# A hybrid RG-LRU and attention block on one core: PSUM reads behind a slot's steps outside the tail, query stores on SyncE, other slots for the odd bank and the gates

## The chip, the core and the metric

The kernel runs on one core of a Trainium2 chip. A core has five engines, each with an instruction queue of its own that it works off in order: TensorE (PE, matrix products into PSUM), VectorE (DVE), ScalarE (ACT), GpSimd (POOL) and SyncE (SP), which here only issues DMAs; ScalarE issues some too. The metric is the time of one execution on the device in microseconds (us), lower is better.

## The reference

One decoder block over 2048 positions of width 1024, in fp32, with these steps (cut):

```
shift, scale, gate = split(silu(c) @ w_mod + b_mod)
h = rms_norm(x) * (1 + scale) + shift
rnn_x, rnn_gate, q, k, v, attn_gate, merge_r, merge_a = split(h @ w_in)      # w_in: 1024 x 8192
y = rg_lru(causal_conv(rnn_x), ...) * silu(rnn_gate)                         # scan along the sequence
o = mixture of three dilated windows of attention(rope(q), rope(k), v) * silu(attn_gate)
m = sigmoid(merge_r) * (y @ w_out_rnn) + sigmoid(merge_a) * (o @ w_out_attn)
out = rms_norm(x + gate * (m @ w_o))
```

## The kernel before

**Products.** The normalized h is held transposed, the sequence in four banks of 512 columns; a half `f` (0 or 1) works on an even and an odd bank. An fp32 product is made of three passes over high and low parts (`mm3`: high x high, high x low, low x high), and ScalarE writes the high part of a weight tile `S`, GpSimd (in the tail of the second half VectorE) the low part: this is a split. Two blocks of rows times two banks are done as one scheme of seven products (`strassen`), in PSUM banks X, Z, W, V, X, Y and V again; the seventh is held back (`behind`) and issued by `last_product` behind the first or second product of the next scheme. One product is twelve matmuls of 128x128 by 128x512, issued by `prod`.

**Order.** There is one order of all instructions, written by hand. `prod` counts products in `n_prod`; a step put into `late[n]` or `after_prod[n]` is issued by `run_late(n)` after product n, and "slot n" of a stage means behind its n-th product (`later(n, fn)`). Each engine receives its instructions in the order in which this code issues them. `prod` also evicts the product (the `evict` that it is given: a copy on ScalarE or a sum on VectorE frees the PSUM bank), loads the next `S` where one is free (`load_free`) and splits the weights that are `ahead` products in front (`split_next`). In the first half the eviction is issued behind the slot's steps, in the second half ahead of them. All DMAs rotate over eight completion semaphores, so one waits in its queue for the one eight before it to land.

**Stages of the second half**, by the span's time: `second_heads` (about 700 to 766 us) runs 20 products, the first and fifth of ten schemes, while `build_odd_late` builds the second half's odd bank: the rows in `x3` are squared and summed on ScalarE (`square`), scaled on VectorE (`scale_rows`, by `rstd_first` and `rstd_last`) and transposed by TensorE from slot 6 on (`ODD_AT`). The gates' stage (`hu`, to 907 us) does the rest of these schemes and sends gates to DRAM through three buffers `ev`; beside it run `residual_gate` (the gate's column sums: loads `gw`, sums `ga`, a row `gateD`) and `rotary_tables` (angles, sines, and four `piece`s: repeat, transpose by TensorE, store). The recurrent stage (`rp`, to 1266 us) does the RG-LRU: gates from small products, sigmoids on ScalarE, the scan on VectorE (L1154), and value blocks, which TensorE transposes (L1356) and ScalarE evicts (L1360). The tail (`qp`, to 1374 us) does a rotated query block, a value block, a rotated key block and two more; beside it `gated_weight` makes four groups of the output weight times the gate (loads `wo`, products with `gb`, sums `ws`, stores to `oD`), and `rotated_pairs` stores rotated queries and keys (`qT`, `kT`). Attention follows from 1374 us.

Lines used below: L163 high part (ScalarE), L169 low part (GpSimd), L172 low part (VectorE), L410 and L411 copies and sums of a scheme, L501 the last sum of a scheme, L561 to L581 building a bank, L894 scaling rows, L1027 squares, L1229 and L1234 a table piece, L1273 to L1309 rotation and its stores, L1339 unrotated query and key stores, L1445 and L1449 gates and their stores, L1511 to L1540 the gated groups.

Of the kernel before, what the change touches and what calls it, by code (L numbers as in the profile page):

```python
# [21 lines left out]
P = 128  # L22
# [68 lines left out]
def decoder_block(ctx, tc, x, c, positions, g_norm, w_mod, b_mod, w_in, b_gate, conv_w, conv_b,  # L91
# [296 lines left out]
    def prod(op, ps, b, first, last, evict):  # L388
        f, i, s = op
        bh, bl = B[b]  # L390
        for k in range(KH):
            mm3(ps[:], s[:, 0, k, :], s[:, 1, k, :], bh[:, k, :], bl[:, k, :],
                first=first and k == 0, last=last and k == KH - 1, skip_group_check=True)
        n_prod[0] += 1
        if f:
            evict()
            used.add(i)
            load_free()
            split_next(i + 4)
        run_late(n_prod[0])  # L400
        if f:
            load_free()
            split_next(i + 4)
        else:
            evict()

    def kept_sum(u, ps, of=None):

# [15 lines left out]
    def strassen(up, f, key, done, u1=None):  # L424

        x, X = pair_id[key], None
        if u1 is None:
            X = T(pj, [P, CH], F32, "X", bufs=2)
            u1 = T(up, [P, CH], F32, "u1", bufs=1)
            prod(take(f, x, 0), X, "B11", True, False, kept_sum(u1, X) if f else last_product)  # L430
            if f:
                last_product()
            else:
                kept_sum(u1, X)()
        Z = T(pj, [P, CH], F32, "Z")
        u2 = T(up, [P, CH], F32, "u2", bufs=2)
        prod(take(f, x, 1), Z, "T2", True, True, kept_sum(u2, Z, u1))
        last_product()
        W = T(pj, [P, CH], F32, "W")
        u3 = T(up, [P, CH], F32, "u3", bufs=1)  # L440
        prod(take(f, x, 2), W, "T3", True, True, kept_sum(u3, W, u2))
        tag = "V" if X is not None else next(body_tags)
        V = T(pj, [P, CH], F32, tag, bufs=1 + (tag == "X"))
        prod(take(f, x, 3), V, "T1", True, False, lambda: done(1, 1, V, u3))
        if X is not None:
            prod(take(f, x, 4), X, "B21", False, True, lambda: done(0, 0, X, None))
        Y = T(pj, [P, CH], F32, "Y")
        prod(take(f, x, 5), Y, "T4", True, True, lambda: done(1, 0, Y, u3))
        op = take(f, x, 6)
        behind.append(lambda: prod(op, V, "B22", False, True, lambda: done(0, 1, V, u2)))  # L450
# [567 lines left out]
    def second_heads(up, st):  # L1018
# [8 lines left out]
            nc.scalar.activation(jk[:], x3[r], AF.Square, accum_out=ss[:, 0, r : r + 1])  # L1027

        for r in range(4):
            plan[1 + r].append(lambda r=r: square(r))  # L1030
        plan[4].append(lambda: rstd_first(ss))
        plan[5].append(lambda: rstd_last(ss))
        plan[5].append(lambda: scale_rows(x3, ss, range(2)))
        plan[6].append(lambda: scale_rows(x3, ss, range(2, 4)))
        for n in ODD_AT:
            plan[n].append(lambda: next(odd))
        for n, fns in plan.items():
# [139 lines left out]
    def rotary_tables(rp, f):  # L1177
# [69 lines left out]
        base = n_prod[0]  # L1247
        for x, fn in enumerate((angles, None, products, *reduce(TWO_PI * 4096, 7, 8), None, *reduce(TWO_PI, 11, 5), quarter, sines)):
            if fn:
                after_prod.setdefault(base + (9 + x if f else TABLES + 7 * (x // 2) + 2 * (x % 2)), []).append(fn)  # L1250

        for x, (q, i) in enumerate((q, i) for q in range(2) for i in range(2)):
            for d, fn in zip((0, 2, 3), piece(q, i)):
                after_prod.setdefault(base + (34 + 3 * x if f else PIECES[x]) + d, []).append(fn)

    def load_tables(qp, f):
        Ct = T(qp, [P, HALF], F32, "Ct")
# [23 lines left out]
    def rotated_pairs(qp, f, Ct, St):  # L1281

        for base, dstT, qs in QK:
            made = [0]

            def rotated(i, j, ps, u, dstT=dstT, qs=qs, made=made):
# [19 lines left out]
                def store():  # L1306
                    for hh in range(4):
                        r0 = (4 * i + hh) * P
                        (nc.scalar if f else nc.sync).dma_start(dstT[r0 : r0 + 32, :, n * P : (n + 1) * P],  # L1309
                                          v[0][hh * 32 : (hh + 1) * 32, :].rearrange("p (r j) -> p r j", r=4))  # L1310

                steps_after(n_prod[0], ((wait, shuffle), (wait + 1, turn), (wait + 2, add), (wait + 3 + f, store)))
# [147 lines left out]
    def later(d, fn):  # L1460

        late.setdefault(n_prod[0] + d, []).append(fn)

    def residual_gate(ep):
# [2 lines left out]
        w, row = {}, {}  # L1467

        def at_slot(i, fn):
            later(i + 6, fn)  # L1470

        def piece():
            return T(ep, [P, CH], F32, "gw", bufs=3)
# [24 lines left out]
        for q in range(2):  # L1498
            for k in range(KT):
                i = KT * q + k  # L1500
                at_slot(i, lambda q=q, k=k: load(q, k))
                at_slot(i + 2, lambda q=q, k=k: add(q, k))
            at_slot(12 + 9 * q, lambda q=q: total(q))
            at_slot(14 + 9 * q, lambda q=q: bias(q))

    O_PART = {"T1": 0, "T2": 1, "T4": 2, "T3": 3, "B11": (0, 0), "B21": (1, 0), "B22": (1, 1)}

    def gated_weight(ep):
# [5 lines left out]
        def group(k):  # L1514
# [23 lines left out]
            def store_sums():  # L1538
                nc.scalar.dma_start(oD[k, :, :2, :], v["t"][:])
                nc.scalar.dma_start(oD[k, :, 2:, :], v[1][:])  # L1540

            return ((0, load), (3, lambda: gate(0)), (4, lambda: gate(1)), (5, lambda: sums(0)),
                    (6, lambda: sums(1)), (7, store_sums))

        for k, i in enumerate((3, 10, 17, 24)):
            for d, fn in group(k):
                later(i + d, fn)

    def next_norm():

# [21 lines left out]
    def next_even():  # L1572
# [19 lines left out]
            later(4 + i, load)  # L1592
        for i in range(NS):
            late.setdefault(N1 + 1 + i - NS, []).append(load_next)
            if i < NS - 3:
                late.setdefault(N1 + 2 + i - NS, []).append(lambda i=i: split_next(i))


    def touch(pool, tags):
# [8 lines left out]
    for f in range(2):  # L1608
# [39 lines left out]
        plain_pool[0] = qp  # L1648
        plain_at[0] = lambda: T(qp, [P, CH], F32, "t0", bufs=NT0)

        touch(qp, (("u1", 1), ("u2", 2), ("u3", 1), ("t0", NT0), ("t1", NT1[f])))
        tabs = load_tables(qp, f)
        if f:
            low_part_by[0] = lo_dve
            gated_weight(qp)
            after_prod.setdefault(N1 + len(ops2) - 7, []).append(load_first_y)
# [886 lines left out]
```

## Time and profile before

| what | value |
|---|---|
| time, median of 3 runs | 2213.46 us (2209.07 to 2214.8) |
| the profiled execution's own time | 2211.68 us |
| its span | 2209.9 us |
| granted TensorE clock, mean | 0.992 |
| TensorE busy | 2158.4 us (98%) |
| VectorE, ScalarE, GpSimd busy | 1523.4, 1261.9, 1205.7 us |
| DMA moved | 510.70 MB, mean 231 GB/s |

A row of a timeline begins with its start and its length in us, then engine, line of the kernel, operation, what it writes `<-` what it reads, the shape and the count of instructions put together. Square brackets give the idle time of that engine ahead of the row and what ended it. "SPq" and "ACTq" are DMA issues on the queues of SyncE and ScalarE. Buffer numbers are left out in the profile.

### The profile page before, as it was taken

What the parts mean: (1) busy time and instruction counts of PE and PEld (TensorE: products, weight loads), DVE (VectorE), ACT (ScalarE), POOL (GpSimd) and SP (SyncE); (2) the same over time, 40 slices, a digit from 0 to 9 for tenths busy, and PEclk for the clock granted to TensorE, in tenths of its full rate; (3) what the DMA queues carried; (4) which work ended last, traced back from release to release, by engine and by line L of the source; (5) the groups of instructions that cost most, each with busy time, mean ns of one, the idle gap of its engine ahead of it and who ended that gap; (6) DMA issues with size and microseconds to landing.
All of it is one profiled execution on the core that took longest, in us unless ns stands there. A gap on an engine that the chain in (4) does not pass through costs nothing. (4 is left out here: it accounts for less than half of the span.)

```text
span 2209.9 us, 33475 instructions
## 1 busy us (share of the span) xinstructions
PE 2158.4 (98%) x10965; PEld 1816.8 (82%) x10965; DVE 1523.4 (69%) x2513; ACT 1261.9 (57%) x2547; POOL 1205.7 (55%) x884
## 2 busy tenths in 40 slices
PE   8999999999999999999999999999999999999998
PEld 6998888888887787888888777888889898978787
DVE  6769788978576854345656668466677778746887
ACT  4547667667534523376766622567677877632443
POOL 2477777677566322355555511356565657433886
PEclk9999999999999999999999999999999999999999
DMA  8355665665986599979784478989888888789653
GB/s 294 110 167 196 212 200 192 204 227 191 269 261 184 147 331 317 289 235 269 241 257 131 129 235 247 290 266 289 275 273 265 246 257 257 229 285 282 190 172 134
DMA packets 455574, 510.70 MB, mean 231 GB/s; under 512 B 91784, under 2 KB 334692, under 8 KB 454632
## 3 DMA queue, kind: packets, MB, share of 16 engines
q1 hardware_dynamic: 423748, 426.30, 64.1%
q10 hardware_dynamic: 31460, 82.22, 9.8%
q8 instruction: 87, 1.43, 0.3%
q14 instruction: 87, 0.71, 0.1%
q0 software_dynamic: 192, 0.05, 0.0%
HBM read 334.38 MB, written 174.07 MB: 230 GB/s over the span
## 5 line engine op out<-in xcount | busy, mean ns | idle before, releaser
L169 POOL TENSOR_TENSOR S<-R,S 128x512 fp32r<-128x512 f32 x254 | 375.7, 1484 | 322.7 <-ACT S L163 272.2
L155 PE MATMUL X<-T,S 128*128 128x512 f32 x1440 | 348.2, 391 | 0.0
L155 PE MATMUL V<-T,S 128*128 128x512 f32 x1344 | 326.7, 392 | 2.1 <-ACT T L163 1.2
L155 PEld LDWEIGHTS X<-T,S 128*128 128x128 f32 x1440 | 270.6, 189 | 56.9 <-issue 0.9
L155 PEld LDWEIGHTS V<-T,S 128*128 128x128 f32 x1344 | 252.1, 189 | 55.5 <-ACT T L163 1.6
L155 PE MATMUL pj<-yh,S 128*128 128x512 f32 x848 | 285.9, 396 | 3.9 <-ACT yh L163 2.6
L169 POOL TENSOR_TENSOR S<-s,S 128x512 fp32r<-128x512 f32 x117 | 186.9, 1598 | 99.8 <-ACT S L163 70.3
L163 ACT ACTIVATE S<-R 128x512 fp32r<-128x512 f32 x266 | 163.8, 621 | 92.7 <-DMA R<-in_w_in_dram 36.2
L155 PEld LDWEIGHTS pj<-yh,S 128*128 128x128 f32 x848 | 159.5, 189 | 37.7 <-ACT yh L163 4.8
L155 PE MATMUL Z<-T,S 128*128 128x512 f32 x768 | 187.6, 394 | 0.0
L155 PE MATMUL W<-T,S 128*128 128x512 f32 x768 | 185.0, 390 | 1.1 <-DVE ev L1445 1.1
L1778 ACT ACTIVATE pp<-pp,st 128x256 f32<-128x256 f32 (+3 forms) x256 | 133.4, 523 | 75.3 <-DVE st L1777 74.7
L155 PE MATMUL Y<-T,S 128*128 128x512 f32 x720 | 173.6, 390 | 0.6 <-POOL S L169 0.6
L155 PEld LDWEIGHTS Z<-T,S 128*128 128x128 f32 x768 | 145.4, 190 | 30.3
L155 PEld LDWEIGHTS W<-T,S 128*128 128x128 f32 x768 | 143.9, 188 | 31.4 <-ACT u1h L410 1.5
L155 PE MATMUL pj<-yl,S 128*128 128x512 f32 x424 | 166.0, 394 | 1.2 <-POOL yl L169 0.9
L155 PEld LDWEIGHTS Y<-T,S 128*128 128x128 f32 x720 | 134.8, 188 | 30.2 <-POOL S L169 1.1
L163 ACT ACTIVATE S<-s 128x512 fp32r<-128x512 f32 x126 | 78.7, 625 | 140.4 <-DVE s L304 44.3
L172 DVE TENSOR_TENSOR ptl<-pT,pth 128x384 fp32r<-128x384 f32 (+1 forms) x160 | 97.8, 628 | 49.2 <-ACT pth L163 46.9
L1777 DVE CUSTOM_DVE_ANT_0 pp<-sc,msk 128x256 f32<-128x256 f32 (+3 forms) x256 | 104.2, 449 | 35.8 <-PE sc L155 33.6
L1842 ACT ACTIVATE pp<-pp,M 128x256 f32<-128x256 f32 (+3 forms) x256 | 118.1, 524 | 9.2 <-DVE M L1966 9.2
L169 POOL TENSOR_TENSOR vh<-vraw,vh 128x256 fp32r<-128x256 f32 (+1 forms) x64 | 66.0, 1031 | 99.4 <-ACT vh L163 77.9
(444 smaller groups left out, 4680.4 us busy)
## 6 DMA issues: line engine op xcount, KB each, us to landing
sD<-S ACTq DMA_DIRECT2D x112, 512.0 KB, 3.7
S<-sD SPq DMA_DIRECT2D x112, 512.0 KB, 5.4
S<-wD SPq DMA_DIRECT2D x100, 512.0 KB, 6.4
R<-in_w_in_dram SPq DMA_DIRECT2D x182, 256.0 KB, 4.0
wD<-s ACTq DMA_DIRECT2D x64, 256.0 KB, 5.2
T<-in_w_mod_dram SPq DMA_DIRECT2D x8, 1024.0 KB
zaT<-ev SPq DMA_DIRECT2D x32, 256.0 KB, 2.9
yaT<-zs SPq DMA_DIRECT2D x32, 256.0 KB, 3.4
```

The costliest lines, as they stand in the source:

```text
L155: nc.tensor.matmul(o, lhsT=l, rhs=r, start=st, stop=sp, **kw)
L163: nc.scalar.activation(o, i, AF.Copy)
L169: nc.gpsimd.tensor_tensor(o, i, h.bitcast(F32), ALU.subtract)
L172: nc.vector.tensor_tensor(o, i, h.bitcast(F32), ALU.subtract)
L1777: nc.vector.tensor_tensor_reduce(pdst, s_ps, mask, 1.0, 3e38, ALU.add, ALU.min, m_)
L1778: nc.scalar.activation(pdst, pdst, AF.Exp, bias=m_, scale=-1.0, accum_out=l_)
L1842: nc.scalar.activation(pp, pp, AF.Copy, scale=w)
```

## The change

It adds and removes no arithmetic and moves instructions only:

1. In the second half `prod` evicts behind the slot's steps too, as the first half did; only in the tail (`tail[0]`) it evicts first. `strassen` likewise.
2. In the 20 products of the heads, splits go 2 products ahead instead of 4; `next_even` makes three first splits at the last three slots instead of four, of which the first was three slots sooner.
3. The odd bank: two squares a slot in slots 1 and 2, scalings in slots 4 and 5 instead of 5 and 6.
4. The second half's rotary tables and their pieces come 8 slots sooner.
5. Rotated queries are stored from SyncE's queue in both halves; keys of the second half stay on ScalarE's.
6. `residual_gate` loads in slots 6 to 28 instead of 6 to 21, adds three slots behind its load instead of two, and makes its sums in slots 21 and 34 instead of 18 and 27.
7. `gated_weight` loads its groups in slots 0, 8, 16, 24 instead of 3, 10, 17, 24, with one more slot between the load and the first product.
8. `touch` sets aside the space of `wo` and `ws` ahead of `Ct`, `St` and `gb`.

```diff
             mm3(ps[:], s[:, 0, k, :], s[:, 1, k, :], bh[:, k, :], bl[:, k, :],
                 first=first and k == 0, last=last and k == KH - 1, skip_group_check=True)
         n_prod[0] += 1
+        if tail[0]:
+            evict()
+        ahead = 2 if i < 2 * N_HEADS else 4
         if f:
-            evict()
             used.add(i)
             load_free()
-            split_next(i + 4)
+            split_next(i + ahead)
         run_late(n_prod[0])
         if f:
             load_free()
-            split_next(i + 4)
-        else:
+            split_next(i + ahead)
+        if not tail[0]:
             evict()
+
+    tail = [False]
 
     def kept_sum(u, ps, of=None):
...
         if u1 is None:
             X = T(pj, [P, CH], F32, "X", bufs=2)
             u1 = T(up, [P, CH], F32, "u1", bufs=1)
-            prod(take(f, x, 0), X, "B11", True, False, kept_sum(u1, X) if f else last_product)
-            if f:
+            prod(take(f, x, 0), X, "B11", True, False, kept_sum(u1, X) if tail[0] else last_product)
+            if tail[0]:
                 last_product()
             else:
                 kept_sum(u1, X)()
...
             nc.scalar.activation(jk[:], x3[r], AF.Square, accum_out=ss[:, 0, r : r + 1])
 
         for r in range(4):
-            plan[1 + r].append(lambda r=r: square(r))
-        plan[4].append(lambda: rstd_first(ss))
-        plan[5].append(lambda: rstd_last(ss))
-        plan[5].append(lambda: scale_rows(x3, ss, range(2)))
-        plan[6].append(lambda: scale_rows(x3, ss, range(2, 4)))
+            plan[1 + r // 2].append(lambda r=r: square(r))
+        plan[3].append(lambda: rstd_first(ss))
+        plan[4].append(lambda: rstd_last(ss))
+        plan[4].append(lambda: scale_rows(x3, ss, range(2)))
+        plan[5].append(lambda: scale_rows(x3, ss, range(2, 4)))
         for n in ODD_AT:
             plan[n].append(lambda: next(odd))
         for n, fns in plan.items():
...
         base = n_prod[0]
         for x, fn in enumerate((angles, None, products, *reduce(TWO_PI * 4096, 7, 8), None, *reduce(TWO_PI, 11, 5), quarter, sines)):
             if fn:
-                after_prod.setdefault(base + (9 + x if f else TABLES + 7 * (x // 2) + 2 * (x % 2)), []).append(fn)
+                after_prod.setdefault(base + (1 + x if f else TABLES + 7 * (x // 2) + 2 * (x % 2)), []).append(fn)
 
         for x, (q, i) in enumerate((q, i) for q in range(2) for i in range(2)):
             for d, fn in zip((0, 2, 3), piece(q, i)):
-                after_prod.setdefault(base + (34 + 3 * x if f else PIECES[x]) + d, []).append(fn)
+                after_prod.setdefault(base + (26 + 3 * x if f else PIECES[x]) + d, []).append(fn)
 
     def load_tables(qp, f):
         Ct = T(qp, [P, HALF], F32, "Ct")
...
                 def store():
                     for hh in range(4):
                         r0 = (4 * i + hh) * P
-                        (nc.scalar if f else nc.sync).dma_start(dstT[r0 : r0 + 32, :, n * P : (n + 1) * P],
+                        (nc.scalar if f and dstT is kT else nc.sync).dma_start(dstT[r0 : r0 + 32, :, n * P : (n + 1) * P],
                                           v[0][hh * 32 : (hh + 1) * 32, :].rearrange("p (r j) -> p r j", r=4))
 
                 steps_after(n_prod[0], ((wait, shuffle), (wait + 1, turn), (wait + 2, add), (wait + 3 + f, store)))
...
         w, row = {}, {}
 
         def at_slot(i, fn):
-            later(i + 6, fn)
+            later(6 + 3 * i // 2, fn)
 
         def piece():
             return T(ep, [P, CH], F32, "gw", bufs=3)
...
                 i = KT * q + k
                 at_slot(i, lambda q=q, k=k: load(q, k))
                 at_slot(i + 2, lambda q=q, k=k: add(q, k))
-            at_slot(12 + 9 * q, lambda q=q: total(q))
-            at_slot(14 + 9 * q, lambda q=q: bias(q))
+            at_slot(10 + 9 * q, lambda q=q: total(q))
+            at_slot(13 + 9 * q, lambda q=q: bias(q))
 
     O_PART = {"T1": 0, "T2": 1, "T4": 2, "T3": 3, "B11": (0, 0), "B21": (1, 0), "B22": (1, 1)}
...
                 nc.scalar.dma_start(oD[k, :, :2, :], v["t"][:])
                 nc.scalar.dma_start(oD[k, :, 2:, :], v[1][:])
 
-            return ((0, load), (3, lambda: gate(0)), (4, lambda: gate(1)), (5, lambda: sums(0)),
-                    (6, lambda: sums(1)), (7, store_sums))
-
-        for k, i in enumerate((3, 10, 17, 24)):
+            return ((0, load), (4, lambda: gate(0)), (5, lambda: gate(1)), (6, lambda: sums(0)),
+                    (7, lambda: sums(1)), (8, store_sums))
+
+        for k, i in enumerate((0, 8, 16, 24)):
             for d, fn in group(k):
-                later(i + d, fn)
+                later(i + d, fn) if i + d else fn()
 
     def next_norm():
...
             later(4 + i, load)
         for i in range(NS):
             late.setdefault(N1 + 1 + i - NS, []).append(load_next)
-            if i < NS - 3:
-                late.setdefault(N1 + 2 + i - NS, []).append(lambda i=i: split_next(i))
+            if i < 3:
+                late.setdefault(N1 + i - 2, []).append(lambda i=i: split_next(i))
 
 
     def touch(pool, tags):
...
         plain_pool[0] = qp
         plain_at[0] = lambda: T(qp, [P, CH], F32, "t0", bufs=NT0)
 
-        touch(qp, (("u1", 1), ("u2", 2), ("u3", 1), ("t0", NT0), ("t1", NT1[f])))
+        touch(qp, (("u1", 1), ("u2", 2), ("u3", 1), ("t0", NT0), ("t1", NT1[f]),
+                   *((("wo", 2, 2, CH), ("ws", 1, 2, CH)) if f else ())))
         tabs = load_tables(qp, f)
         if f:
+            tail[0] = True
             low_part_by[0] = lo_dve
             gated_weight(qp)
             after_prod.setdefault(N1 + len(ops2) - 7, []).append(load_first_y)
```

The order written out shows what this moves at three places. In the first, VectorE late in the recurrent stage, `y<-a,htail` is the scan, `u<-Z` and `u<-W` are evictions of products of the scheme that runs then. Before:

```order
L317 TENSOR_TENSOR s_2150_11447<-R_2144_11418,s_2150_11447 128x512
L411 TENSOR_TENSOR u_2178_11589<-Z_11588,u_2167_11531 128x512
L1153 TENSOR_TENSOR t_11515<-t_11515,gi_11469 128x512
L1154 SCALAR_TENSOR_TENSOR y_11468<-a_11514,htail_199,t_11515 128x512
L411 TENSOR_TENSOR u_2184_11616<-W_11615,u_2178_11589 128x512
L1159 TENSOR_TENSOR zs_11337<-y_11468,zs_11337 128x512
```

After:

```order
L317 TENSOR_TENSOR s_2150_11446<-R_2144_11417,s_2150_11446 128x512
L505 TENSOR_TENSOR ev_11585<-V_11453,u_2142_11398 128x512
L1157 TENSOR_TENSOR t_11513<-t_11513,gi_11467 128x512
L1158 SCALAR_TENSOR_TENSOR y_11466<-a_11512,htail_199,t_11513 128x512
L415 TENSOR_TENSOR u_2178_11589<-Z_11588,u_2167_11531 128x512
L1163 TENSOR_TENSOR zs_11351<-y_11466,zs_11351 128x512
L415 TENSOR_TENSOR u_2184_11616<-W_11615,u_2178_11589 128x512
```

The scan and the product ahead of it now stand in front of the eviction of Z, and the last eviction of V stands behind L317.

The second place is ScalarE in the tail; `t<-pg` are evictions of transposed values, `qT<-t` stores of rotated queries, `oD` the stores of the first gated group. Before:

```order
L163 ACTIVATE S_2261_11979<-s_2241_11848 128x512
L1539 DMA oD<-ws_11951 128x1024
L1540 DMA oD<-wo_11845 128x1024
L1309 DMA qT<-t_2250_11907 128x1x128 x4
L1309 DMA qT<-t_2254_11930 128x1x128 x4
L1273 ACTIVATE t_2274_12053<-X_11913 128x512
L410 ACTIVATE u_2284_12092<-X_12091 128x512
L1309 DMA qT<-t_2269_12013 128x1x128 x4
L1360 ACTIVATE t_2285_12112<-pg_12083 128x512
L1360 ACTIVATE t_2290_12139<-pg_12115 128x512
L1309 DMA qT<-t_2276_12058 128x1x128 x4
L1360 ACTIVATE t_2294_12168<-pg_12142 128x512
```

After:

```order
L1543 DMA oD<-ws_11911 128x1024
L1544 DMA oD<-wo_11801 128x1024
L163 ACTIVATE S_2263_11968<-R_2204_11719 128x512
L1282 ACTIVATE t_2260_11957<-t_2260_11957 128x512
L163 ACTIVATE S_2266_11988<-s_2244_11851 128x512
L1277 ACTIVATE t_2277_12056<-X_11920 128x512
L414 ACTIVATE u_2287_12096<-X_12095 128x512
L1364 ACTIVATE t_2289_12118<-pg_12087 128x512
L1364 ACTIVATE t_2293_12144<-pg_12121 128x512
```

The sixteen stores of queries are gone from this queue, and the stores to `oD` come two splits sooner.

The third place is SyncE's queue at the same time; the three `S` loads in a row are those of the rotated key's first products. Before:

```order
L1511 DMA gb_11794<-gateD 128x1024
L260 DMA R_2235_11826<-in_w_in_dram 128x4x128
L1521 DMA wo_11843<-in_w_o_dram 128x1024
L1521 DMA wo_11845<-in_w_o_dram 128x1024
L339 DMA S_2262_11982<-sD 128x1024
L339 DMA S_2263_11984<-sD 128x1024
L339 DMA S_2266_12001<-sD 128x1024
L1521 DMA wo_12005<-in_w_o_dram 128x1024
L1521 DMA wo_12007<-in_w_o_dram 128x1024
L339 DMA S_2272_12031<-sD 128x1024
```

After:

```order
L1515 DMA gb_11797<-gateD 128x1024
L1525 DMA wo_11799<-in_w_o_dram 128x1024
L1525 DMA wo_11801<-in_w_o_dram 128x1024
L260 DMA R_2240_11833<-in_w_in_dram 128x4x128
L1525 DMA wo_11961<-in_w_o_dram 128x1024
L1525 DMA wo_11963<-in_w_o_dram 128x1024
L339 DMA S_2267_11991<-sD 128x1024
L339 DMA S_2268_11993<-sD 128x1024
L339 DMA S_2271_12010<-sD 128x1024
L1313 DMA qT<-t_2254_11914 128x1x128 x4
L339 DMA S_2275_12034<-sD 128x1024
L1313 DMA qT<-t_2258_11938 128x1x128 x4
```

The second group's `wo` loads have moved from behind the three `S` loads to ahead of them, the first group's ahead of the raw load `R`, and the query stores stand between later `S` loads.

## Prediction

> **What bounds the kernel now.** The first line of the page gives the span, the row of busy times the engines, and these two show that TensorE is the bound:
>
> ```profile
> span 2209.9 us, 33475 instructions
> PE 2158.4 (98%) x10965; PEld 1816.8 (82%) x10965; DVE 1523.4 (69%) x2513; ACT 1261.9 (57%) x2547; POOL 1205.7 (55%) x884
> ```
>
> TensorE works for 2158.4 of 2209.9 us, so only its 51.5 us of waiting can be won by moving other engines' work. Next I asked what TensorE waited for between 680 us (end of the first half) and 1380 us (attention has begun), where every edit lies:
>
> ```profile
> PE pg L1356 <- ACT t L1360: 4.8, 1, 4.8
> PE pg L1356 <- ACT y L1129: 3.4, 2, 1.9
> PE pg L561 <- DVE T L894: 2.5, 3, 1.3
> PE pj L155 <- ACT yh L163: 2.0, 1, 2.0
> PE pg L1234 <- DVE ev L1229: 1.8, 1, 1.8
> PE pg L1356 <- ACT sg L1360: 1.7, 1, 1.7
> PE pg L561 <- DVE t L581: 1.5, 2, 0.7
> PE V L155 <- ACT T L163: 1.2, 1, 1.2
> PE W L155 <- DVE ev L1445: 1.1, 1, 1.1
> ...
> ```
>
> Columns: who waited, for whom, us in total, times, longest. These nine make 20.0 us. A longer wait costs more than itself, as three stretches of the table by stretches show, right behind waits of 1.9, 4.8 and 1.8 us (the number after POOL's count is the clock granted to TensorE), and the products in them:
>
> ```profile
> 1252.40:1257.30 4.90, 4.84 (x17) 3.92 (x18) 0.00 (x0) 1.18 (x3) 1.29 (x1) 0.65 0.16 59
> 1315.90:1322.00 6.10, 6.07 (x17) 4.96 (x18) 0.00 (x0) 1.06 (x2) 0.00 (x0) 0.52 1.05 279
> 870.00:873.00 3.00, 3.00 (x16) 2.53 (x17) 1.12 (x2) 1.25 (x2) 0.85 (x1) 1.00 1.04 409
> 1252.87 4.58 PE L155 MATMUL V<-T,S 128*128 128x512 f32 x12
> 1263.11 3.02 PE L155 MATMUL V<-T,S 128*128 128x512 f32 x12
> 1316.70 5.33 PE L155 MATMUL Z<-T,S 128*128 128x512 f32 x12
> ```
>
> Twelve matmuls behind transposes take 3.02 us at full clock (1263.11), but 4.58 and 5.33 where the clock was 0.65 and 0.52: 1.6 and 2.3 us more. The Trainium skill ("TensorE: Matmul & The Clock Gate", HAM oscillation) gives as rule that TensorE should have no idle gaps above about 3.4 us. By that rule the wait of 1.9 would not slow what follows, its 1.6 us would not come back, and the sum below would be -17.1 in place of -18.7; the row has the clock at 0.65 behind 1.9 us and at 1.00 behind 1.8, so here the rows decide.
>
> **The change part by part.** No arithmetic is added or removed; every term is a wait. Durations are those of the profiled execution, 2211.68 us (2209.9 and 1.8 around it), which is 1.8 below the median of the runs shown.
>
> *Later splits at the turn of the halves.* The two waits for DVE t (1.5 us) stand behind ScalarE's splits, which wait for raw loads in front of the next bank's build, as in the second of two places:
>
> ```profile
> 693.82 0.63 ACT L163 ACTIVATE S<-R 128x512 fp32r<-128x512 f32 x1 [4.18 <-DMA R<-in_w_in_dram]
> ```
>
> The change puts three splits at the last slots in place of four up to three slots sooner, so the builds no longer stand behind a load that is on its way: -1.5.
>
> *Odd bank scaled sooner.* In slot 6 the transposes wait for the scaling, and the scaling had been waiting for the squares:
>
> ```profile
> 712.90 1.05 ACT L1027 ACTIVATE t<-T 128x1024 bf16<-128x1024 f32 x1
> 715.72 4.78 DVE L894 TENSOR_SCALAR T<-T,ss 128x1024 f32<-128x1024 f32 x4
> 717.13 0.27 PE L561 MATMUL pg<-cs,T 128*128 128x128 f32 x1
> 725.50 0.60 PE L561 MATMUL Y<-cs,T 128*128 128x128 f32 x4
> 729.15 0.60 PE L561 MATMUL pg<-cs,T 128*128 128x128 f32 x4
> ```
>
> Slot 6 takes 725.50 - 717.13 = 8.37 us, slot 7, which has as many transposes, 3.65: a loss of 4.7. Two squares to a slot end the last square some 6 us sooner (four of some 1.2 us with the reading of the sum, between 702 and 708, two evictions among them), and VectorE, idle there, ends its four scalings of 1.2 at about 714, where slot 6 now begins at 715.6. The whole 4.7 comes back: -4.7.
>
> *Steps before evictions, outside the tail.* The recurrence's scan stands behind the eviction of Z on VectorE, ScalarE waits for the scan, then loads a table and evicts the bank that TensorE's transposes need:
>
> ```profile
> 1243.99 0.63 ACT L1149 ACTIVATE t<-t 128x512 f32<-128x512 f32 x1
> 1248.88 1.28 DVE L1154 TENSOR_TENSOR_SCAN y<-a,htail,t 128x512 f32<-128x512 f32 x1
> 1250.20 0.20 ACT L1157 ACTIVATE htail<-y 128x1 f32<-128x1 f32 x1 [3.57 <-DVE y L1154]
> ```
>
> With the scan ahead of Z's eviction, the square root (done at 1244.6) and VectorE's work before it set it: it ends near 1248.1 instead of 1250.2, and the transposes wait 0.1 in place of 1.9. The other wait of this kind (3.4 - 1.9 = 1.5) goes likewise; of that for sg (1.7), which stands behind VectorE's eviction of V, I take half. Here: 1.5 + 1.8 + 1.6 (clock) + 0.9 = -5.8. What is late next are the evictions; nothing reads the Z bank for five products. That the order as such is harmless can be read in the first half, which has had it always; in 70 to 680 us TensorE's longest wait was this:
>
> ```profile
> PE V L155 <- DVE xr L501: 0.5, 1, 0.5
> ```
>
> *Rotated queries stored by SP.* ScalarE issues 16 stores of queries, and its evictions stand behind them until buffers have landed:
>
> ```profile
> 1299.84 7.00 ACTq L1309 DMA_DIRECT2D qT<-t  x8
> 1306.95 0.60 ACT L1273 ACTIVATE t<-X 128x512 f32<-128x512 f32 x1 [9.19 <-DMA qT<-t]
> 1315.28 0.60 ACT L1360 ACTIVATE t<-pg 128x512 f32<-128x512 f32 x1 [6.70 <-DMA qT<-t]
> ```
>
> TensorE's transposes need the bank that ScalarE frees with the eviction at 1315.28. Off that queue ScalarE can do it at about 1308.5, when it waits only for a t0 buffer that VectorE frees: -4.85 - 2.3 = -7.2. The 16 issues (eight took 7.00 us on ScalarE) now lie on SP's queue, behind the loads of S for the rotated key's first three products and ahead of later ones.
>
> *Gated groups.* Group 1's two loads now stand on SP ahead of three loads of S, and the second of them waits until group 0's store has landed:
>
> ```profile
> 1298.76 0.68 DVE L1536 TENSOR_TENSOR wo<-wo,ws 128x512 f32<-128x512 f32 x1
> 1288.41 8.48 SPq L339 DMA_DIRECT2D S<-sD  x3
> DMA to landing us min/median/max: 3.0/6.4/8.4
> DMA to landing us min/median/max: 6.6/6.6/6.6
> 1290.93 2.88 PE L155 MATMUL Z<-T,S 128*128 128x512 f32 x12
> 1304.89 3.00 PE L155 MATMUL X<-T,S 128*128 128x512 f32 x12
> ```
>
> Group 0's last sum (1298.76) comes nine instructions of about 0.7 sooner, near 1292.5; its store is landed 3.0 to 6.4 us later by the first row on landing (1295.5 to 1299), the loads of S are issued some 0.5 us after and land 6.6 later by the second: 1302.6 to 1306, against need at 1304.9. An added wait, then: between 0 and 1.2 + 2.3 (clock) = 3.5; the middle is just in time, I take +0.5. VectorE's first gating now stands ahead of two low parts of S and waits for wo: issued near 1276 and landed 6.6 later, as S is, so that the parts are done by 1288, and the product that reads the first of them begins at 1290.93. At the end of the tail the wait for yh (2.0) is for this store buffer; the space now lies elsewhere, but the last store is a slot later: between 0 and -2.0, I take -1.0.
>
> *Split-ahead of 2 instead of 4 in the heads.* VectorE has hardly a gap there, and splits of S wait on ScalarE behind its work:
>
> ```profile
> 730.60:766.00 35.40, 33.06 (x149) 26.83 (x148) 34.75 (x42) 21.82 (x39) 12.34 (x9) 1.00 0.51 146
> ```
>
> Between 0 and +4.7 (the two waits of 1.1 and 1.2 there, twice more), I take +1.0; most products find their split a product early.
>
> *Gate sums and tables.* Same loads, spread over 22 slots for 15; tables move eight slots forward, where three ev buffers are shared with gates whose stores land late. At the old place:
>
> ```profile
> 868.86 0.96 DVE L1229 COPY ev<-co 128x512 f32<-128x512 f32 x1 [2.85 <-ACT ev L1440]
> ```
>
> Between -1.8 (the wait for ev goes) and +5.4 (all four table pieces wait 1.8): I take 0, between the two, since the buffers are as scarce at the new place, by the row at the slower rival.
>
> Sum: -1.5 - 4.7 - 5.8 - 7.2 + 0.5 - 1.0 + 1.0 + 0 = -18.7 us. 2211.68 - 18.7 = 2193.0; against the median 2213.46 - 18.7 = 2194.8. I say 2194.
>
> **Rivals.** *The heads give back the scaling's gain.* For it speaks VectorE's full queue and the halved lead; against it that the same number of splits runs, one to a product. Four products late by 1.2 us take back 4.7, and the later clock some 1.5: -18.7 + 5.2 = -13.5, 2200.
>
> *The queries' stores do no less harm on SP.* SP's queue is in order, and its stores wait for VectorE; a load of S or a raw load behind them is then late. If the 7.2 stays and S is late by its 3.5, the change is -18.7 + 7.2 + 3.0 = -8.5: 2204.
>
> *The change doesn't take the waits away*: they are only handed to the next releaser, since the evictions come later by a slot's steps. If the scan's and the turn's terms stay as well, -8.5 + 7.3 = -1.2: 2212, no change.
>
> *Slower: evictions too late in the gates' stage (766 to 907 us).* VectorE waits there for ev buffers, as here:
>
> ```profile
> 865.32 0.69 DVE L501 TENSOR_TENSOR ev<-Y,u 128x512 f32<-128x512 f32 x1 [4.12 <-DMA gaT<-ev]
> ```
>
> Behind the steps of a slot, with table pieces taking ev buffers among them, each eviction comes later still. It decides once an eviction lags more than the five products, 13.6 us, until Z's bank is used again; the row shows a lag of 4. If eight of these waits reach TensorE with 3.5 us and 1.5 of clock each, +40: 2211.7 - 18.7 + 40 = 2233.
>
> **How the numbers follow.** The forecast has 0.60 (2187 to 2200), the heads 0.14, SP 0.12, no change 0.08, slower 0.06. What a measurement of this kernel tells from no change is about 0.3%, 6.6 us. The sum with every term at its best is -1.5 - 4.7 - 6.6 - 7.2 - 2.0 - 1.8 = -23.8 from the profiled execution, 2188; the range begins at 2186 and reaches past the third case to 2208, which leaves out the last two and a little below. Faster: the first two, and most of SP's case, 0.82; same: the rest of it and no change, 0.12; slower 0.06.
>
> **What would show it.** Right: no wait for T at slot 6, none for t from ScalarE in the tail, ScalarE's evictions there without a query store in front, clock 1.00 in the stretches quoted; the stretch from 700 to 766 some 5 us shorter, the one from 1266 to 1374 some 8. Wrong: X of the rotated key waiting for S from DMA, V or W in the heads waiting for ScalarE or GpSimd more than 2.4 us in all, transposes of tables waiting more than 1.8.

## The result and the profile after

| | before | after |
|---|---|---|
| median | 2212.83 us (2209.07 to 2214.8, 4 runs) | 2193.71 us (2189.85 to 2195.43, 4 runs) |
| profiled execution | 2211.68 us | 2189.85 us |

The ratio is 0.9913, with a 95% interval of 0.9894 to 0.9932: faster by 19.1 us between the medians, where 18.7 were forecast (2194). The two profiled executions lie 21.8 us apart, since that of after is the fastest of its four. One profiled execution below (the odd bank's slots alone, first time) ran at a mean clock of 0.654 and took 3051.59 us; its trace is not read and its time is in no median.

The page of after, its span and its row of busy times:

```profile
span 2188.1 us, 33499 instructions
PE 2153.4 (98%) x10964; PEld 1813.8 (83%) x10965; DVE 1520.4 (69%) x2513; ACT 1265.1 (58%) x2547; POOL 1196.8 (55%) x884
```

TensorE's work is 5.0 us less (slow products that are gone), its idle time 34.7 us instead of 51.5. The waits of TensorE after the change from 670 to 1370 us, all of them:

```profile
PE V L155 <- ACT T L163: 1.7, 1, 1.7
PE pj L155 <- ACT yh L163: 1.6, 2, 1.2
PE pg L1238 <- DVE ev L1233: 1.3, 1, 1.3
PE sc L155 <- POOL kq L169: 1.0, 1, 1.0
PE pj L155 <- DMA S<-wD: 0.4, 1, 0.4
PE X L155 <- POOL S L169: 0.3, 1, 0.3
PE pg L1360 <- ACT sg L1364: 0.3, 1, 0.3
PE X L155 <- DVE S L172: 0.2, 1, 0.2
PE V L155 <- DVE t L505: 0.2, 1, 0.2
```

7.0 us, where the nine rows of before made 20.0: both waits for y, that for T at the odd bank, those for t at the turn and that for t from ScalarE (4.8) are no longer there. The clock granted to TensorE, which stands behind POOL's count, is 1.00 in all four stages (the heads, the gates' stage, the recurrent stage, the tail; the bounds are set by eye, so lengths are read from the table below):

```profile
700.00:760.00 60.00, 57.95 (x269) 47.07 (x268) 46.26 (x56) 38.03 (x67) 26.05 (x18) 1.00 0.48 142
760.00:900.00 140.00, 138.73 (x614) 112.70 (x613) 63.27 (x107) 38.68 (x60) 31.00 (x23) 1.00 0.99 324
900.00:1255.00 355.00, 354.55 (x1586) 293.02 (x1585) 211.10 (x236) 235.91 (x383) 189.13 (x136) 1.00 0.71 218
1255.00:1358.00 103.00, 101.06 (x449) 81.88 (x448) 79.17 (x121) 28.95 (x52) 14.10 (x10) 1.00 0.83 258
```

Where the time came from is read by laying the starts of the same matmuls of the two traces side by side:

| at | before | after | difference so far |
|---|---|---|---|
| first transposes of slot 6 | 717.13 | 714.20 | -2.9 |
| first transposes of slot 7 | 725.50 | 717.81 | -7.7 |
| end of the heads (Z) | 766.48 | 758.98 | -7.5 |
| end of the gates' stage (V) | 907.78 | 897.97 | -9.8 |
| end of the recurrent stage (Z) | 1271.89 | 1255.66 | -16.2 |
| tail, ahead of the transposes (X) | 1299.09 | 1282.90 | -16.2 |
| tail, two products behind them (W) | 1321.87 | 1297.96 | -23.9 |
| tail, last V | 1371.32 | 1348.24 | -23.1 |
| products with yh | 1384.98 | 1361.35 | -23.6 |
| attention, 65 us on | 1448.99 | 1427.14 | -21.9 |
| last products | 2193.85 | 2172.00 | -21.9 |

Three places make up most of the gain: slot 6 (-4.8), the recurrent stage (-6.4) and the tail's transposes (-7.7). The gates' stage adds -2.3, and some 2 us are given back behind the tail. In slot 6 the last square starts at 702.90 instead of 712.90, the scalings end at 711.99 (707.12 + 4.87) instead of 720.5, and the transposes wait for nothing:

```profile
702.90 1.05 ACT L1031 ACTIVATE t<-T 128x1024 bf16<-128x1024 f32 x1
707.12 4.87 DVE L898 TENSOR_SCALAR T<-T,ss 128x1024 f32<-128x1024 f32 x4
714.20 1.03 PE L565 MATMUL pg<-cs,T 128*128 128x128 f32 x8
714.99 2.99 PE L155 MATMUL X<-T,S 128*128 128x512 f32 x12
717.81 0.60 PE L565 MATMUL Y<-cs,T 128*128 128x128 f32 x4
```

In the tail ScalarE's two evictions end at 1293.4 with no store in front, and the transposes of the same block, with the product behind them, run without a gap and at full clock (3.02 us for 5.33):

```profile
1292.30 1.08 ACT L1364 ACTIVATE t<-pg 128x512 f32<-128x512 f32 x2
1294.76 0.60 PE L1360 MATMUL pg<-cs,t 128*128 128x128 f32 x4
1295.11 3.02 PE L155 MATMUL Z<-T,S 128*128 128x512 f32 x12
```

### The profile page after: what moved, and what is told of

Read it like the earlier page. It is cut to its first block, busy times and chain, and to the rows that moved or that the text cites. A ratio compares the mean times of both kernels' runs of the same rounds, so it can differ in the third digit from the quotient of the medians.

```text
span 2188.1 us, 33499 instructions
## 1 busy us (share of the span) xinstructions
PE 2153.4 (98%) x10964; PEld 1813.8 (83%) x10965; DVE 1520.4 (69%) x2513; ACT 1265.1 (58%) x2547; POOL 1196.8 (55%) x884
## 5 line engine op out<-in xcount | busy, mean ns | idle before, releaser
L1120 DVE SCALAR_TENSOR_TENSOR xc<-xr,par,xc 128x512 f32<-128x512 f32 x96 | 104.1, 1085 | 47.2 <-ACT xc L1114 44.9
```

The costliest lines, as they stand in the source:

```text
L1120: nc.vector.scalar_tensor_tensor(xc, xr[:, i : i + CH], cw(i), xc, ALU.mult, ALU.add)
```

## The experiments

All are after with a part undone, or before with a part done alone. Ratios are to the kernel before on the same chip (medians 2213.19, 2211.42 and 2211.41 us in the three rounds). Places are compared by the starts of the same matmuls, as in the table above.

### What brought the odd bank's 4.8 us

The slots of edit 3 undone, all else as after:

```diff
-            plan[1 + r // 2].append(lambda r=r: square(r))
-        plan[3] ... plan[4] ... plan[4] ... plan[5]
+            plan[1 + r].append(lambda r=r: square(r))
+        plan[4] ... plan[5] ... plan[5] ... plan[6]
```

> The changed kernel with the odd bank's squares, rstd and scaling in their old slots. Theory: slot 6 of the heads takes 4.7 to 4.8 us longer (2.5 of waits for scaled rows, the rest a product at a reduced clock), and nothing later gives it back: about 2198.5. Rival (VectorE's full queue limits the heads, so the head start is lost again there): slot 6 is longer, but the waits behind it at W and V shrink, and less than 2 us are left by the end of the heads.

Measured: 2196.12 us, ratio 0.9925 (0.9908 to 0.9941). The expected 2198.5 did not come: the wait that should be back is a tenth of what it was (2.5 us). Its wait, then ScalarE's last square and the eviction of the slot's own product behind it, and last that eviction in before:

```profile
PE pg L565 <- DVE T L898: 0.3, 1, 0.3
706.97 1.05 ACT L1031 ACTIVATE t<-T 128x1024 bf16<-128x1024 f32 x1
708.67 0.60 ACT L414 ACTIVATE u1h<-W 128x512 f32<-128x512 f32 x1
711.88 0.60 ACT L410 ACTIVATE u1h<-W 128x512 f32<-128x512 f32 x1 [0.52 <-PE W L155]
```

The square of the old slot 4 starts 5.9 us before that of the kernel before (712.90), while slot 6 itself is only some 3 sooner. The reason stands in ScalarE's rows: before, the square (712.90) is behind the eviction of the slot's own product (`u1h`, 711.88), which waits until TensorE has ended it; with edit 1 the square (706.97) is ahead of that eviction (708.67). So edit 1 does alone what edit 3 was credited with. Edit 1 alone (shown below) shortens slot 6 by 4.3 us: 2.77 at the transposes and 1.50 at the product behind them, which runs at full clock. The other direction is edit 3 alone, the same lines put into before, first by its time:

> The kernel before with one part of the change: the odd bank's squares, rstd and scaling in their new slots. Theory (either the order or the slots suffice for slot 6, so the gain was claimed by one and would have come by the other): slot 6 is 4 to 4.7 shorter, the waits for T gone or under 0.5, about 2208.5. Rival (the slots alone don't do it, with evictions still ahead of the squares): under 1.5.

The median is 2208.55 us, ratio 0.999 (0.9978 to 1.0003): near the 2208.5 that was expected, but not told apart from no change by time. The same kernel, by its trace:

> The kernel before with edit 3 alone, once more, for a profile of slot 6 of the heads. Theory (either the sooner slots or the evictions behind the steps is enough for the odd bank): the first of slot 6 to the first of slot 7 takes 3.6 to 4.4 us for 8.37, and the waits of transposes for T add to 0.5 us at most. Rival (the slots alone do little, since evictions in front of the squares still hold them up): slot 6 takes 6.5 us or more and waits for T stay above 1.5.

```profile
714.65 0.49 PE L561 MATMUL pg<-cs,T 128*128 128x128 f32 x3
715.47 0.76 PE L561 MATMUL pg<-cs,T 128*128 128x128 f32 x5 [0.33 <-DVE T L894]
718.81 0.60 PE L561 MATMUL Y<-cs,T 128*128 128x128 f32 x4
```

Slot 6 takes 718.81 - 714.65 = 4.2 us (before 8.37) and waits 0.3. Either edit is enough for this wait; the two together win it once. Its time in this one run was 2204.11.

### Evictions behind the steps, and the gate's sums

Edit 1 undone (evictions ahead of the steps in all of the second half):

```diff
-        if tail[0]:
+        if f:
             evict()
```

> The changed kernel with evictions ahead of the slot's steps in all of the second half. Theory (the scan stood behind the eviction of Z): the waits for y and sg of the recurrent stage come back, 1.5, 1.9 with a half-clock product of 1.6 more, and 1.5: some 6.5 us, about 2200; the gates' stage loses what it won without being forecast (2.1 us) only if the order did that too, and then the total is 8.6. Rival (the recurrent stage gained since everything before it came sooner against the loads): under 2 us.

2206.57 us, ratio 0.9968 (0.9952 to 0.9984): of the 19 us, 12.9 are lost, where 6.5 to 8.6 were expected. The waits of before are back in the recurrent stage, and a larger one in the gates' stage, at the table pieces that edit 4 has moved there:

```profile
PE pg L1238 <- DVE ev L1233: 7.4, 2, 4.6
PE pg L1360 <- ACT y L1133: 3.4, 2, 2.0
PE pg L1360 <- ACT sg L1364: 1.7, 1, 1.7
```

In its profiled execution, which is 18.5 us above after's, the gates' stage is 9.5 us longer, the recurrent stage 4.8, the tail 2.1 and what lies ahead of the gates' stage as much. Then edit 1 alone, put into before:

> The kernel before with one part of the change: evictions behind the slot's steps outside the tail. The runs so far suggest that this order also moves the odd bank's squares one product forward, ahead of the evictions that wait for TensorE. Theory: it alone gives the 4.7 of slot 6 less 0.3, the 6.5 of the recurrent stage and some 2 in the gates' stage: -13, about 2200. Rival (slot 6 was won by the new slots of squares and scaling, which this kernel doesn't have): -6.5 to -8.5, about 2205.5, with the waits for T of 2.5 still there.

2205.12 us, ratio 0.9967 (0.9956 to 0.9977). That is half of the 13 us expected. It is near the rival's number, but not by the rival's way: the waits for T at slot 6 are gone (0.3 left). The recurrent stage gains 6.3 us and slot 6 its 4.3, but the gates' stage loses 7.2 at one product and the next (4.9 over the whole stage, since smaller waits there are gone). TensorE's row and VectorE's two, and then VectorE's same two in before:

```profile
835.07 5.49 PE L155 MATMUL X<-T,S 128*128 128x512 f32 x12 [4.44 <-DVE ev L505]
832.86 0.75 DVE L1489 SCALAR_TENSOR_TENSOR ga<-gw,ca,ga 128x512 f32<-128x512 f32 x1 [4.01 <-DMA gw<-in_w_mod_dram]
834.34 0.68 DVE L505 TENSOR_TENSOR ev<-X,u 128x512 f32<-128x512 f32 x1
832.60 0.69 DVE L501 TENSOR_TENSOR ev<-X,u 128x512 f32<-128x512 f32 x1
837.70 0.75 DVE L1485 SCALAR_TENSOR_TENSOR ga<-gw,ca,ga 128x512 f32<-128x512 f32 x1 [4.41 <-DMA gw<-in_w_mod_dram]
```

A sum of the gate waits 4.01 us for its load `gw`, as it did in before (4.41). There the eviction of X stands ahead of it; here it stands behind it, and TensorE needs that bank. That is what edit 6 moves. After with edit 6 alone undone:

```diff
-            later(6 + 3 * i // 2, fn)
+            later(i + 6, fn)
...
-            at_slot(10 + 9 * q, lambda q=q: total(q))
-            at_slot(13 + 9 * q, lambda q=q: bias(q))
+            at_slot(12 + 9 * q, lambda q=q: total(q))
+            at_slot(14 + 9 * q, lambda q=q: bias(q))
```

> The changed kernel with edit 6 undone: the gate's column sums load one piece to every slot from 6 to 21 and add two slots behind their load. Theory (edit 6 is what pays for the evictions behind the steps: an add that waits some 4 us for its load now holds up the eviction behind it): X waits for VectorE's ev about 4.4 us near 835 us, products behind it are 2.6 slower, 7 us in all, about 2200.5 us. Rival (that wait came from the tables' place or from chance in the loads): 0 to 2 us, at most 2195.5, and no wait of X for ev over 1 us in the gates' stage.

2200.06 us, ratio 0.9954 (0.9939 to 0.9969), 6.4 above after's median. The same pair of rows:

```profile
833.37 5.34 PE L155 MATMUL X<-T,S 128*128 128x512 f32 x12 [4.77 <-DVE ev L505]
831.36 0.75 DVE L1489 SCALAR_TENSOR_TENSOR ga<-gw,ca,ga 128x512 f32<-128x512 f32 x1 [4.41 <-DMA gw<-in_w_mod_dram]
```

Against after, the start of that X falls 4.94 us further behind and that of the next product another 2.46; by 847 us 7.1 are left of it, about the theory's 7. Edit 6 alone in before was not run. There the wait for `gw` reaches no product, so the edit has nothing to win at that place; with edit 1 it saves those 7. Edit 4, the tables, undone:

```diff
-                ... base + (1 + x if f else ...)
-                ... base + (26 + 3 * x if f else ...)
+                ... base + (9 + x if f else ...)
+                ... base + (34 + 3 * x if f else ...)
```

> The changed kernel with the rotary tables and their pieces back at their old slots. Putting evictions first cost 9.4 us in the gates' stage with the tables sooner, while the kernel before, with the tables later, lost only 1.8 there. Theory (the tables' new slots are where the ev buffers are scarcest, and only the new order of evictions keeps this from costing): the wait of 1.3 for a piece goes, -1 to 0: 2193 to 2194. Rival (the tables' slots won the 2.1 us that the gates' stage gained): +1 to +2.

2193.85 us, ratio 0.9924 (0.9907 to 0.9941): not told apart from after. Its pieces wait for nothing, but an eviction does, so the 1.3 of the one is exchanged for the 1.4 of the other:

```profile
PE V L155 <- DVE ev L505: 1.4, 1, 1.4
```

### Queries on SyncE's queue, and the gated groups

Edit 5 undone (rotated queries stored by ScalarE again):

```diff
-                        (nc.scalar if f and dstT is kT else nc.sync).dma_start(
+                        (nc.scalar if f else nc.sync).dma_start(
```

> The changed kernel with the rotated queries' stores back on ScalarE's queue, all else as changed. Theory (the stores in ScalarE's queue held up the evictions that TensorE's transposes need): the wait for t in the tail comes back with 4 to 5 us and the half-clock product behind it with 2 to 2.5, so the stretch from the rotated key's first transposes to its W product is 7.2 us longer and the kernel about 2201. Rival (the gated groups, moved in the same tail, made room on VectorE and on the buffers, and the queue mattered little): under 2 us, about 2195.

2198.51 us, ratio 0.9936 (0.9922 to 0.995), 4.8 above after. TensorE's two waits in the tail, and for the second of them ScalarE's eviction behind eight stores:

```profile
PE pg L1360 <- ACT t L1364: 2.2, 1, 2.2
PE pg L1360 <- ACT t L1277: 1.5, 1, 1.5
1284.77 10.13 ACTq L1313 DMA_DIRECT2D qT<-t  x8
1295.00 0.60 ACT L1277 ACTIVATE t<-X 128x512 f32<-128x512 f32 x1 [9.63 <-PE X L155]
```

The issues of the stores end at 1294.90 and the eviction begins at 1295.00. The wait for ScalarE's t is back, split in two (3.7 us for before's 4.8), and the products behind both take 3.0 us, so no slow clock comes with it. So the ScalarE queue is the cause, and its price is 4 to 6 here instead of 7. Edit 5 alone, put into before:

> The kernel before with one part of the change: rotated queries stored from SyncE's queue. Theory as predicted: the wait for t (4.85) and the half-clock product behind it (2.3) both go, -7.2, about 2206. Rival from the first run, where putting them back cost only 4.1 to 6.5 in the tail: the eviction on ScalarE would still come late, since VectorE frees its t0 buffer late with the old slots of the gated groups; -4 with a wait of 1 to 2 us left.

2216.69 us, ratio 1.0026 (1.0015 to 1.0037): slower than before by 5, where the theory and its rival both expected a gain. The wait for ScalarE's t goes, with 7.7 us, as in after; then TensorE loses more than that. TensorE's row, VectorE's, two of SyncE's queue, and last the same loads in before:

```profile
1343.04 5.46 PE L155 MATMUL V<-T,S 128*128 128x512 f32 x12 [5.46 <-DVE t L501]
1336.91 1.23 DVE L1524 TENSOR_TENSOR wo<-wo,gb 128x1024 f32<-128x1024 f32 x1 [6.25 <-DMA wo<-in_w_o_dram]
1325.35 3.13 SPq L1309 DMA_DIRECT2D qT<-t  x4
1330.42 0.92 SPq L1521 DMA_DIRECT2D wo<-in_w_o_dram  x2
1323.45 6.83 SPq L1521 DMA_DIRECT2D wo<-in_w_o_dram  x2
```

SyncE issues the loads of the third group's `wo` at 1330.42, behind the query stores, where before it began at 1323.45. VectorE waits 6.25 us for them, and the last sum of V, eight instructions behind, comes when TensorE has waited 5.46. A load of `S` is late here too, by 0.8 us at one product (0.7 in the next run). Edits 7 and 8 undone in after should then show the same:

```diff
-            return ((0, load), (4, ...), (5, ...), (6, ...), (7, ...), (8, store_sums))
+            return ((0, load), (3, ...), (4, ...), (5, ...), (6, ...), (7, store_sums))
-        for k, i in enumerate((0, 8, 16, 24)):
+        for k, i in enumerate((3, 10, 17, 24)):
...
-                   *((("wo", 2, 2, CH), ("ws", 1, 2, CH)) if f else ())))
```

> The changed kernel with edits 7 and 8 undone: the gated groups load in slots 3, 10, 17 and 24 again, one slot less between load and product, and their space lies where it was; the queries stay on SyncE's queue. Theory (the two edits are a pair: with the queries' stores on SyncE's queue, a group that loads at the old slots comes behind them, its loads land late, VectorE waits for them with the last sum of a product behind it): a wait of V for VectorE's t of about 5.5 us comes back near 1340 us, with some 2.5 of slower products, about 2201.5 us, and VectorE's sums of the third group wait 5 us or more for the load of wo. Rival (the changed kernel's other edits leave room for that wait): 0 to 2 us, at most 2195.5, and no wait for t over 1 us.

2200.4 us, ratio 0.9955 (0.9941 to 0.9969), 6.7 above after:

```profile
1325.11 4.58 PE L155 MATMUL V<-T,S 128*128 128x512 f32 x12 [4.21 <-DVE t L505]
1318.99 1.23 DVE L1528 TENSOR_TENSOR wo<-wo,gb 128x1024 f32<-128x1024 f32 x1 [5.04 <-DMA wo<-in_w_o_dram]
```

The start of this V falls 4.37 us further behind after's, that of the next product another 1.70. The wait is at the predicted instruction; it came some 15 us sooner than "near 1340", which had been taken from a trace that runs later. Last, the three edits together in before:

> The kernel before with edits 5, 7 and 8 alone: rotated queries stored by SyncE, gated groups loaded sooner, their space set aside first. Theory (a pair): the wait for t from ScalarE goes with its slow products, 7.2 to 7.7 us, and no wait for wo reaches TensorE, so about 2204 to 2205 us. Rival (what the stores gain is given back later in the tail whatever the groups' slots): -2 to +4 us, as with the stores alone (2216.7 beside 2211.4), and a wait of V for VectorE's t of several us near 1343.

2206.93 us, ratio 0.9978 (0.9965 to 0.999): a gain, of 4.5 instead of the 7. In the tail the theory holds: -5.01, -0.41 and -2.32 at the transposes and the two products behind, and no wait for `wo` reaches TensorE. From there to the end of the execution 6.2 of 10.4 us are given back: most of it at attention's start, where TensorE now waits for what GpSimd and DMAs prepare, and 1.7 in its last stage:

```profile
PE Z L155 <- DVE yh L2096: 4.0, 1, 4.0
PE sc L155 <- POOL q L1740: 3.1, 5, 1.4
PE pj L155 <- DMA S<-wD: 1.3, 1, 1.3
```

Why Z waits 4.0 there was not followed further; after has 2.5 at the same place and loses nothing net.

### Splits two products ahead

Edit 2 undone:

```diff
-        ahead = 2 if i < 2 * N_HEADS else 4
+        ahead = 4
...
-            if i < 3:
-                late.setdefault(N1 + i - 2, []) ...
+            if i < NS - 3:
+                late.setdefault(N1 + 2 + i - NS, []) ...
```

> The changed kernel with splits 4 products ahead everywhere and the old first splits at the turn of the halves. Theory: the two waits for t at the turn (0.7 each) come back, 1.5 to 2.1 us; in the heads the waits of 1.7 for T and 0.3 for S from GpSimd go away or become the 1.1 and 1.2 of before, so the heads change by -1 to +0.5: total +0.5 to +2, which the time hardly shows, 2194 to 2196. Rival (the shorter lead is what lets the heads keep VectorE free for the odd bank): heads 2 us longer or more, 2198.

2196.9 us, ratio 0.9927 (0.9913 to 0.9941). A small wait at the turn of the halves is there again (its row below), the heads are 0.8 shorter, and by 760 us the trace stands level with after's:

```profile
PE pg L565 <- DVE t L585: 0.9, 2, 0.8
```

The 3.2 us between the medians are inside what the runs scatter, and this edit's worth, if any, stays open. The trace is still 0.6 us ahead of after's at 1361 us and ends 4.2 behind: all of that comes in attention, whose code is the same. With the tables at their old slots it is the same there (0.5 ahead, 4.0 behind), so attention alone differs by up to 4.8 us between profiled executions of kernels with the same code there.

## Why the prediction was right, and where it was not

The total and the direction came out, and the main mechanism too: evictions and steps that wait for each other in in-order queues. That the medians lie 19.1 us apart, within 0.4 of the sum, is in part luck: the places below make 21.9 between the two profiled executions, with terms missed both ways, and the medians have only four runs each. By its own steps:

- **Turn of the halves, -1.5.** About -2.2 between the two profiled executions. But this wait is not steady: it is 1.5 us in the profiled execution of before, 0.7, 0.2 and none in three other kernels with the same code there (odd bank alone; queries and groups; queries alone). The term took one execution's wait for the kernel's.
- **Odd bank, -4.7.** -4.8: the size is right. The step that failed is the attribution: "Two squares to a slot end the last square some 6 us sooner" is one of two sufficient causes, and edit 1 alone gives 4.3. It was costed as if the other edits did not touch the squares. Of the 4.8, some 1.5 are a slow product that need not come (below).
- **Steps before evictions, -5.8.** -6.4 in the recurrent stage. The scan moved as told; y's waits went wholly, and that for sg fell by 1.4 instead of the half that was taken. TensorE's transposes and the product behind them, at full clock:

```profile
1239.21 0.66 PE L1360 MATMUL pg<-cs,ev 128*128 128x128 f32 x4
1239.62 3.00 PE L155 MATMUL V<-T,S 128*128 128x512 f32 x12
```

- **Rotated queries, -7.2.** -7.7 at the place, and the end of the wait was shown by undoing and by doing alone. What failed is the price of the other side: the stores are placed "behind the loads of S for the rotated key's first three products and ahead of later ones", and nothing is put down for the groups' `wo` behind them. Without edits 7 and 8 the edit is a loss of 5 us. The rival on SyncE's queue named S and raw loads as what comes late; the runs show `wo`, with 6.25 and 5.04 us of waiting, and S with 0.8 and 0.7.
- **Gated groups, +0.5, and yh, -1.0.** The added wait for the rotated key's S did not come: in after, its first three products (X, V and Z, at 1288.70 to 1295.11) wait for nothing. yh gave -0.5, and undoing edits 7 and 8 costs 1.4 there. But the groups' edit is worth 6.7 by the run without it, as cover for edit 5.
- **Heads, +1.0.** +0.2: a wait for T grew to 1.7 and one of 0.3 for GpSimd's S came, one for ev of 1.1 went. The rival that the heads give the gain back did not occur.
- **Gate sums and tables, 0.** The gates' stage came out 2.3 shorter, a little beyond the term's best of -1.8, and not by the tables: with them at their old slots the waits of their pieces are gone too, as they are with edit 1 alone. For the tables 0 is what the run showed. For the sums it was wrong in kind: without edit 6 the stage is 7 us longer. The slower rival had the place and the mechanism (evictions too late in the gates' stage) but named the stores of `ev` as what VectorE waits for, with eight such waits; it is the load of `gw`, at one product, and it happens as soon as edit 1 is made without edit 6.
- **Attention gives back 1.8.** Not in the sum. It starts 23.6 us sooner, and the trace has waits of 1.0 us for GpSimd's kq and 1.2 for its queries at 1367 and 1372 us. The 1.8 are less than what attention differs between the profiled executions above.

So the sum was right as a sum over the whole change, and wrong as a list of what each edit is worth. Between the medians the single undoings cost 12.9, 6.7, 6.4, 4.8, 3.2, 2.4 and 0.1 us (edits 1, 7 with 8, 6, 5, 2, 3, 4), some 36 together for a gain of 19.1. By the ratios, each to the kernel before in its own round, they are 12, 9, 9, 5, 3, 3 and 2 us, and the intervals of the last four overlap that of after: time alone tells a loss only for edits 1, 7 with 8, and 6, and for edit 5 the waits do. Edits 7 and 8 were undone only together. Edits 6, 7 and 8 are covers: the waits that they prevent, for `gw` and `wo`, do not reach TensorE in before, which has none of the edits; they come with edits 1 and 5. No version tried is faster than after; the one with the tables at their old slots is not told apart from it.

## What to carry to other kernels

An edit that moves work past something in an in-order queue is costed by everything that then stands behind it, up to the next instruction that a bottleneck engine waits for: here a sum that waits 4 us for its load cost nothing until an eviction was put behind it, and 7 us after that. When several edits come together, cost them in pairs, since one may hold the slack that another needs; undoing each alone and doing each alone tells gains from covers. A wait of one or two microseconds in one profiled execution is not yet a property of the kernel.

## What the runs showed of the clock

The prediction read from two rows that the clock falls behind a wait of 1.9 us and not behind 1.8. That did not hold. The same transposes, behind the same wait, in the kernel with the queries and groups alone:

```profile
1250.87 0.66 PE L1356 MATMUL pg<-cs,ev 128*128 128x128 f32 x4 [1.95 <-ACT y L1129]
1251.28 3.01 PE L155 MATMUL V<-T,S 128*128 128x512 f32 x12
```

3.01 us at full clock, where before has 4.58 behind 1.92. Over the thirteen readable traces, from 690 to 1350 us:

| TensorE waits | times | twelve matmuls behind take |
|---|---|---|
| 1.45 to 1.80 us | 23 | 2.97 to 3.01 us, always full clock |
| 1.92 to 2.22 us | 9 | 4.58 us in two (1.92, 1.93), about 3.0 in seven |
| 2.80 to 5.46 us | 9 | 3.96 to 5.49 us, always slow |

The table counts each wait singly, and shorter ones add up: at slot 6 three waits of 0.83, 1.34 and 0.33 us within some 3 us stand in front of one product. It takes 4.50 us in before, 4.58 with the queries and groups alone, and 2.99 with the queries alone.

So the 1.5 us for slot 6's slow product, and the 1.6 us for the slow product in the recurrent stage's term, are a matter of the execution; the latter was there in before's profiled execution and in one other of the five traces that have this wait of 1.9 to 2.0. Waits of 2.80 us and longer cost 0.9 to 2.5 us more than themselves, against the 3.02 at full clock. The Trainium skill ("TensorE: Matmul & The Clock Gate", HAM oscillation) puts the limit at about 3.4 us of idling: the rows at 2.80 and at 1.92 are slow below it, so it is too generous a limit here. The same page of the Trainium skill ("What's actually happening") says that the window over which the activity is watched runs freely, so that the number of slow matmuls at a kernel's start changes from run to run; the two outcomes at 1.9 to 2.2 us would fit that, but no run here shows the window.
